# Position terms taken out of the compression's input and added to its product; the two widest HGRN2 spans subtracted by ScalarE's bias

## The chip, the cores and the metric

The kernel runs on one core of a Trainium2 chip. Five engines work side by side: TensorE (PE) multiplies, VectorE (DVE) and ScalarE (ACT) work element by element, GpSimd (POOL) issues the indirect gathers, and SyncE (SP) issues nearly all other transfers. The metric is the device time of one execution in microseconds (us).

## The reference, cut to what matters

One decoder layer over 1024 tokens of width 1024: RMSNorm, one wide input projection, three parallel mixers (stick-breaking attention, native sparse attention with a compressed, a selected and a sliding branch, HGRN2 recurrence), a gated merge, then a PEER expert layer with 16384 experts, and a last RMSNorm. Two places of it are touched:

```python
# native sparse attention: keys and values compressed over blocks of 32 tokens, stride 16
def compress(x, w):
    pieces = x.reshape(B, G, n_piece, CMP_STRIDE, dh)
    blocks = jnp.concatenate([pieces[:, :, j:j + n_cmp] for j in range(per)], axis=3) + cmp_pe
    return blocks.reshape(B, G, n_cmp, CMP_LEN * dh) @ w

# HGRN2, inside one chunk: the decay between two times
b = jnp.cumsum(gc, axis=2)
rel = b[:, :, :, None, :] - b[:, :, None, :, :]
decay = jnp.exp(jnp.where(causal[:, :, None], rel, -jnp.inf))
```

`cmp_pe` is one array of 32 x 64 position terms, the same for every block, so `(blocks + cmp_pe) @ w` is `blocks @ w` plus one vector of 64 numbers.

## The kernel before, in words

The tokens go through in four parts of 256. For each part the kernel writes out the normalisation, the projections (`proj`: 24 matmuls per block of 128 columns, each operand split into two fp16 halves), and the *items* of the mixers, which are stepped through a four-stage software pipeline: for each part and each of four rounds one HGRN2 head (`hg_items`), one tile of sparse attention (`nsa_items`) and one pair of stick-breaking heads (`sb_items`). The other work (projections, merges, output projection, PEER scores and routes) is cut into pieces, and a planner places them between the items: it adds up a modelled DVE and PE load of what has been written so far (`account`) and keeps each at so much per step (`RDVE`, `RPE`). The tile framework then schedules all of it by a timeline of its own, and that fixes the order of each engine's queue. So an edit of a few instructions moves many others.

PEER is done in two ways. Parts 1 and 2 (512 tokens) are computed densely, in 128 blocks of experts, after the mixers (`gemm1`, `gemm2`, here *the dense stage*). Each block takes 24 matmuls of 512 columns into `g`, 18 into the six `acc` banks, and every fourth block 24 more for the seventh and eighth bank, whose sum DVE adds at L1451. Parts 0 and 3 (512 tokens, four tiles of 128) go by gathers: POOL fetches for each of 128 ranks one row of 4 KB per token, 0.524 MB in all, first from the table `u` (L1149, multiplied by DVE at L1151), then from `v` (L1159, accumulated by DVE at L1161 into `gacc`). That makes 1024 gathers and 1024 DVE instructions. 420 of them are spread over the mixers' steps by `paced`, and the rest are left to the scheduler in the dense stage. A gather row needs a free buffer, so a gather is issued when DVE has finished with an earlier row.

The changed places:

- `pieces(which)`, for keys (0) and values (1) of each part. `plain` projects the block and ACT copies it out of PSUM into `xc` (L486). `add_pe` then lets DVE write `xp`, of 16 position pairs by group by compressed block, with the position term added, in four instructions (group by parity) for each half of the 32 positions (L510), and four small ones for the piece carried over from the part before (`xhist`, stored at L521). Every token is written twice, once in each half.
- `compress(which, dst)`: 16 fp32 matmuls over `xp` into `pk` (L526), copied by DVE into `kcT` or `vcT` (L527).
- `level(lv)` of `hg_items`, seven levels for each of 16 head-parts. For level `lv` the 256 columns are cut into spans of `2w`, `w = 2**lv`; `spans` subtracts from each span the value of `b` at its middle, by one DVE instruction of 128 x 256 (L806), and ACT takes the absolute value (L807) and the exponential (L808).

The order of queues that matters for what follows: each engine works through its own queue in order; DVE's queue in the mixers holds HGRN2, attention, route and gather instructions mixed, and in the dense stage the weight splits `us` and `vs` (L221), the gating `ge` (L1434), the split `ac`, the bank sums and the gathers' instructions.

## Time and profile before

| what | us |
|---|---|
| median of 3 runs | 3500.18 (3494.5 to 3507.36) |
| the profiled execution | 3511.97 |
| its span, first to last instruction | 3510.2 |
| PE busy | 3199.7 |
| DVE busy | 3000.6 |
| ACT busy | 1556.4 |
| POOL busy | 1361.7 |

The profiled execution took 1.8 us more than its span, and 11.8 us more than the median of the runs. Mean granted TensorE clock: 0.942. Times within the trace count from the span's start. In rows of windows, what stands behind each stretch is its length, then the busy time of each engine with the number of instructions, the granted clock, the mean busy share of the 16 DMA engines, and GB/s. In rows of groups, the count is followed by the busy time of all, the mean of one in ns, and the idle time of the engine just before them with what ended it.

### The profile page before, as it was taken

To read this page: it belongs to the slowest core of one execution; us is meant where nothing else is said; L and a number is where in the kernel's file an instruction comes from. 1 tells how busy PE (TensorE), PEld (TensorE's weight loads), DVE (VectorE), ACT (ScalarE), POOL (GpSimd) and SP (SyncE) were. 2 spreads that over 40 slices of the span, in tenths; PEclk is the share of its full clock that TensorE was granted. 3 is DMA by queue.
4 is the path that set the end of the run, shared out by engine and by line. 5 is a ranking of instruction groups with operands and counts; after the bars stand their busy time and mean duration, and the time that the engine had idled before them with its cause. 6 is when DMAs were issued, how large, how long until landed. Compare 5 with 4: busy or idle time off the path is not lost.

```text
span 3510.2 us, 56907 instructions
## 1 busy us (share of the span) xinstructions
PE 3199.7 (91%) x20564; PEld 2175.3 (62%) x20564; DVE 3000.6 (85%) x6666; ACT 1556.4 (44%) x3181; POOL 1361.7 (39%) x1170
## 2 busy tenths in 40 slices
PE   7999889999997799999887889889999999999998
PEld 6887777778886688888565745434444444444443
DVE  6665679888789879889997869999988998998998
ACT  5776455554543554554455233333333333333333
POOL 0000002443332322333231334357765565676672
PEclk9999999999997799999688999989999999999999
DMA  8964856889976588897574998789999999999995
GB/s 305 334 248 147 308 185 226 320 314 310 358 284 231 199 289 291 327 332 259 191 250 154 344 372 312 241 271 387 392 384 329 385 367 362 362 368 375 367 358 219
DMA packets 359283, 1058.00 MB, mean 301 GB/s; under 512 B 35236, under 2 KB 107573, under 8 KB 354391
## 3 DMA queue, kind: packets, MB, share of 16 engines
q0 software_dynamic: 147456, 536.94, 42.5%
q1 hardware_dynamic: 206934, 483.87, 38.7%
q10 hardware_dynamic: 4608, 33.56, 2.5%
q8 instruction: 161, 2.64, 0.3%
q14 instruction: 124, 1.01, 0.1%
HBM read 944.13 MB, written 110.10 MB: 300 GB/s over the span
## 4 chain that ended last, share of the span: by engine, by line
PE 49%; DVE 23%; DMA 11%; issue 8%; ACT 6%; POOL 2%; SPq 0%; DVEq 0%; POOLq 0%; ACTq 0%
PE g L265 13%; PE acc L1441 10%; PE pj_mg L265 4%; DVE u L1151 3%; DVE gacc L1161 3%; PE g L1441 3%; DMA u<-in_peer_u_dram,gidx 3%; PE pj_r_hg L265 2%; DMA v<-in_peer_v_dram,gidx 1%; PE pb L265 1%; DMA gt<-d_G 1%; PE pj_wo L265 1%; POOL v L1159 1%; PE z_sb L417 1%; DMA vraw<-in_peer_v_dram 1%
## 5 line engine op out<-in xcount | busy, mean ns | idle before, releaser
L1159 POOL DMA_INDIRECT v<-in_peer_v_dram,gidx x421 | 556.0, 1321 | 674.0 <-DVE gacc L1161 348.4
L1149 POOL DMA_INDIRECT u<-in_peer_u_dram,gidx x417 | 529.7, 1270 | 596.6 <-DVE u L1151 367.4
L265 PE MATMUL g<-h,us 128*128 128x512 f16 x3072 | 688.2, 381 | 14.8 <-ACT ge L1400 12.1
L1441 PE MATMUL acc<-vs,ac 128*128 128x512 f16 x2304 | 542.2, 383 | 39.9 <-ACT vs L220 23.5
L1441 PEld LDWEIGHTS <-ac 128*128 128x128 f16 x3072 | 303.1, 99 | 426.1 <-issue 66.8
L1161 DVE SCALAR_TENSOR_TENSOR gacc<-v,act,gacc 128x1024 f32<-128x1024 f32 x421 | 538.9, 1280 | 29.4 <-DMA v<-in_peer_v_dram,gidx 25.8
L265 PEld LDWEIGHTS <-us 128*128 128x128 f16 x3072 | 301.6, 98 | 383.0 <-issue 21.1
L1151 DVE SCALAR_TENSOR_TENSOR u<-u,gh 128x1024 f32<-128x1024 f32 x417 | 501.9, 1219 | 33.2 <-DMA u<-in_peer_u_dram,gidx 32.7
L1400 ACT ACTIVATE ge<-g 128x512 f32<-128x512 f32 x128 | 76.1, 596 | 520.7 <-PE g L265 500.1
L265 PE MATMUL pj_mg<-hT,w_mg 128*128 128x256 f16 x2304 | 273.8, 275 | 4.0 <-ACT mg L885 4.0
L265 PEld LDWEIGHTS <-w_mg 128*128 128x128 f16 x2304 | 228.2, 100 | 33.6 <-issue 6.6
L1441 PE MATMUL g<-vs,ac 128*128 128x512 f16 x768 | 190.5, 388 | 11.6 <-ACT ge L1400 11.6
L1149 POOL DMA_INDIRECT rr_u<-in_peer_u_dram,gidx x95 | 134.2, 1413 | 96.7 <-DVE rr_u L1151 49.8
L221 DVE SCALAR_TENSOR_TENSOR vs<-vraw,vs 128x1024 f16<-128x1024 f32 x128 | 154.1, 1219 | 18.6 <-ACT vs L220 18.5
L221 DVE SCALAR_TENSOR_TENSOR us<-uraw,us 128x1024 f16<-128x1024 f32 x128 | 156.1, 1219 | 10.4 <-ACT us L220 10.3
L265 PE MATMUL pb<-o,w_b 128*128 128x256 f16 x1152 | 144.7, 281 | 21.1 <-DVE sg L923 15.1
L1159 POOL DMA_INDIRECT rr_v<-in_peer_v_dram,gidx x90 | 123.0, 1367 | 102.2 <-DVE gacc L1161 81.4
L220 ACT ACTIVATE vs<-vraw 128x1024 f16<-128x1024 f32 x128 | 131.0, 1046 | 55.0 <-DMA vraw<-in_peer_v_dram 55.0
L220 ACT ACTIVATE ac<-ge 128x512 f16<-128x512 f32 x128 | 79.9, 628 | 168.3 <-DVE ge L1434 139.0
L1434 DVE TENSOR_TENSOR ge<-ge,gt 128x256 f32<-128x256 f32 x256 | 98.4, 422 | 58.7 <-ACT ge L1400 44.9
L1223 PE MATMUL gb<-hot 128*128 128x128 f16 x512 | 125.7, 294 | 24.3 <-ACT stage L1226 13.1
L220 ACT ACTIVATE us<-uraw 128x1024 f16<-128x1024 f32 x128 | 134.2, 1048 | 21.4 <-PE g L265 12.8
(1146 smaller groups left out, 6353.8 us busy)
## 6 DMA issues: line engine op xcount, KB each, us to landing
uraw<-in_peer_uT_dram SPq DMA_DIRECT2D x128, 512.0 KB, 7.7
vraw<-in_peer_v_dram SPq DMA_DIRECT2D x128, 512.0 KB, 7.2
w_mg<-dw SPq DMA_DIRECT2D x72, 512.0 KB, 5.8
gt<-d_G SPq DMA_DIRECT2D x32, 1024.0 KB, 17.5
d_G<-stages ACTq DMA_DIRECT2D x20, 1024.0 KB, 5.9
w_r_hg<-dw SPq DMA_DIRECT2D x36, 512.0 KB, 5.4
w_b<-dw SPq DMA_DIRECT2D x72, 256.0 KB, 5.5
wr_mg<-in_wblk_dram SPq DMA_DIRECT2D x24, 512.0 KB, 5.3
```

Source lines behind the costliest of these rows:

```text
L220: S.activation(hi, src, AF.Copy, scale=scale)
L221: V.scalar_tensor_tensor(lo, in0=src, scalar=scale, in1=hi, op0=ALU.mult, op1=ALU.subtract)
L265: P.matmul(ps, l[:, k, :], r[:, k, :], start=(i == 0), stop=(i == n - 1))
L417: P.matmul(x["z"], qz[:, hh, tl * 128:(tl + 1) * 128], st["k"][:, r0 + c0:r0 + c1], start=True, stop=(c0 > 0))
L1149: G.indirect_dma_start(out=ur, out_offset=None, in_=a["peer_u"], in_offset=bass.IndirectOffsetOnAxis(ap=idx[:, c:c + 1], axis=0))
L1151: V.scalar_tensor_tensor(ur, in0=ur, scalar=1.0, in1=h2, op0=ALU.mult, op1=ALU.mult, accum_out=hpre[:, c:c + 1])
L1159: G.indirect_dma_start(out=vr, out_offset=None, in_=a["peer_v"], in_offset=bass.IndirectOffsetOnAxis(ap=idx[:, c:c + 1], axis=0))
L1161: V.scalar_tensor_tensor(acc, in0=vr, scalar=act[:, c:c + 1], in1=acc, op0=ALU.mult, op1=ALU.add)
L1223: P.matmul(ps[:, n, :], hs[:, 0, :, n], hs[:, 2, :, n], start=True, stop=False)
L1400: S.activation(ge, ps, AF.Gelu, scale=1.0 / (SW * SH2))
L1434: V.tensor_tensor(gv, gv, gt[:, :, i % 8, :], op=ALU.mult)
L1441: P.matmul(ps, ac[:, x, t * 128:(t + 1) * 128], v[:, y, dh * 512:(dh + 1) * 512], start=start and n == 0, stop=stop and n == 2)
```

## The change

The position terms are laid out on the host as 16 columns of 128 (`pos`) in place of 32 columns of 64 written twice. `pieces` keeps its projection in PSUM, and ACT writes it straight into `xp` with four instructions of 64 x 8 x 16; `xp` now holds each token once (8 position pairs, one column more), and the matmuls of the second half read it one column further on. The carried piece is copied by ACT, in and out of `xhist`. On the first part the 16 weight blocks are also multiplied with `pos` (16 more matmuls of one column for keys, 16 for values), DVE copies the result to `cpos`, and the copy of `pk` becomes an addition of `cpos`. In `level`, where there are four spans or fewer (levels 5 and 6), ACT computes the absolute difference itself, one instruction for each span with the middle value as its bias.

The words given for the change name a third part, ranks decoded by eleven VectorE operations. The diff holds no edit of the decoding: in both kernels `route` decodes with the same 26 instructions per tile (L1038 to L1052 before).

```diff
-    small = load(cst.tile([128, 40], F32, name="small"), a["small"])
-    peT, hnorm, hlb = small[:, 0:32], small[:, 32:36], small[:, 36:40]
+    small = load(cst.tile([128, 24], F32, name="small"), a["small"])
+    pos, hnorm, hlb = small[:, 0:16], small[:, 16:20], small[:, 20:24]
...
-    xhist = per.tile([128, 2, 16], F32, name="xhist")
+    xhist = per.tile([128, 2, 8, 2], F32, name="xhist")
+    cpos = per.tile([64, 2], F32, name="cpos")
...
         def pieces(which):
-            plain(B_NKV + which, f"xc{which}")
-            xc = st[f"xc{which}"]
-            xp = st["xp", which] = W2(f"xp{which}_{nm}", (128, 16, 2, np_), tag="xp", bufs=1)
-
-            def add_pe(half, d0, nb, src):
-                for g in range(2):
-                    gs = slice(g * 64, g * 64 + 64)
-                    for par in range(2):
-                        o = xp[par * 64:par * 64 + 64, half * 8:half * 8 + 8, g, d0:d0 + nb]
-                        i = src[gs].rearrange("p (c j u) -> p u j c", j=8, u=2)[:, par]
-                        e = peT[gs, half * 16:half * 16 + 16].rearrange("p (j u) -> p u j", u=2)[:, par]
-                        V.tensor_tensor(o, i, e.unsqueeze(2).to_broadcast([64, 8, nb]), op=ALU.add)
-            if pt.first:
-                add_pe(0, 0, np_ - 1, xc[:, 0:n - 16])
-                add_pe(1, 0, np_ - 1, xc[:, 16:n])
-            else:
-                add_pe(0, 0, 1, xhist[:, which, :])
-                add_pe(0, 1, np_ - 1, xc[:, 0:n - 16])
-                add_pe(1, 0, np_, xc)
+            ps = proj(B_NKV + which, hTs[pt.i], f"xc{which}_{nm}", pt)
+            d0 = 0 if pt.first else 1
+            xp = st["xp", which] = W2(f"xp{which}_{nm}", (128, 8, 2, np_ + 1), tag="xp", bufs=1)
+            if not pt.first:
+                S.activation(xp[:, :, :, 0], xhist[:, which], AF.Copy)
+            for g in range(2):
+                for par in range(2):
+                    o = xp[par * 64:par * 64 + 64, :, g, d0:d0 + np_]
+                    S.activation(o, ps[g * 64:g * 64 + 64].rearrange("p (c j u) -> p u j c", j=8, u=2)[:, par], AF.Copy, scale=PS)
             if not pt.last:
-                V.tensor_copy(xhist[:, which, :], xc[:, n - 16:n])
+                S.activation(xhist[:, which], xp[:, :, :, d0 + np_ - 1], AF.Copy)
 
         def compress(which, dst):
             pk = ps_mm.tile([64, 2, np_], F32, tag="mm", name=f"pk{which}_{nm}")
             for j in range(16):
-                P.matmul(pk[:, :, 0:ncb], st["cw", which][:, j, :], st["xp", which][:, j, :, 0:ncb], start=(j == 0), stop=(j == 15))
-            V.tensor_copy(dst[0:64, :, c0:c1], pk[:, :, 0:ncb])
+                P.matmul(pk[:, :, 0:ncb], st["cw", which][:, j, :], st["xp", which][:, j % 8, :, j // 8:j // 8 + ncb], start=(j == 0), stop=(j == 15))
+            if pt.first:
+                pc = ps_mm.tile([64, 1], F32, tag="mm", name=f"pc{which}")
+                for j in range(16):
+                    P.matmul(pc, st["cw", which][:, j, :], pos[:, j:j + 1], start=(j == 0), stop=(j == 15))
+                V.tensor_copy(cpos[:, which:which + 1], pc)
+            V.tensor_scalar(dst[0:64, :, c0:c1], pk[:, :, 0:ncb], cpos[:, which:which + 1], None, op0=ALU.add)
...
             def spans():
                 y["X"] = X = W2(f"X{lv}_{nm}", (128, n))
-                b4 = halves(x["b"])
-                V.tensor_tensor(halves(X), b4, b4[:, :, 0:1, w - 1:w].to_broadcast([128, ns, 2, w]), op=ALU.subtract)
-                S.activation(X, X, AF.Abs)
+                if ns <= 4:
+                    for i in range(0, n, 2 * w):
+                        S.activation(X[:, i:i + 2 * w], x["b"][:, i:i + 2 * w], AF.Abs, scale=-1.0, bias=x["b"][:, i + w - 1:i + w])
+                else:
+                    b4 = halves(x["b"])
+                    V.tensor_tensor(halves(X), b4, b4[:, :, 0:1, w - 1:w].to_broadcast([128, ns, 2, w]), op=ALU.subtract)
+                    S.activation(X, X, AF.Abs)
                 S.activation(X, X, AF.Exp, scale=-1.0)
```

The queues are scheduled anew, and three places of them are shown. In the rows a tile's name ends in the number of its buffer, and the lines of the changed kernel are up to six lower for the same statement (one higher near L221).

First, DVE in part 2, at the compression of the keys. `xc` and `xp` are the projection and its rearranged copy, `u` a gathered row, `o` and `e_sb` belong to the attention of part 1. Before:

```order
L1151 SCALAR_TENSOR_TENSOR u_70_32828,hpre_32615<-u_70_32828,gh_0_32609 128x1024
L510 TENSOR_TENSOR xp_ns_9666<-xc_ns_9664,small 64x8x15 x4
L510 TENSOR_TENSOR xp_ns_9666<-xc_ns_9664,small 64x8x16 x4
L521 COPY xhist<-xc_ns_9664 128x16
L1151 SCALAR_TENSOR_TENSOR u_71_32831,hpre_32615<-u_71_32831,gh_0_32609 128x1024
L429 SCALAR_TENSOR_TENSOR e_sb_1_1_0_0_9531<-r_sb_1_1_0_0_9534,e_sb_1_1_0_0_9531 128x512
L221 SCALAR_TENSOR_TENSOR o_1_7834<-tro_ns1g_0_9542,o_1_7834 128x256
L1151 SCALAR_TENSOR_TENSOR u_72_32834,hpre_32615<-u_72_32834,gh_0_32609 128x1024
L221 SCALAR_TENSOR_TENSOR o_1_7834<-tro_ns1g_1_9547,o_1_7834 128x256
L527 COPY kcT<-pk_ns_9744 64x2x16
L510 TENSOR_TENSOR xp_ns_9820<-xhist,small 64x8 x4
```

And in the change:

```order
L1149 SCALAR_TENSOR_TENSOR u_75_32846,hpre_32618<-u_75_32846,gh_0_32612 128x1024
L1149 SCALAR_TENSOR_TENSOR u_76_32849,hpre_32618<-u_76_32849,gh_0_32612 128x1024
L222 SCALAR_TENSOR_TENSOR o_1_7853<-tro_ns1g_0_9565,o_1_7853 128x256
L222 SCALAR_TENSOR_TENSOR o_1_7853<-tro_ns1g_1_9570,o_1_7853 128x256
L430 SCALAR_TENSOR_TENSOR e_sb_1_1_0_0_9554<-r_sb_1_1_0_0_9557,e_sb_1_1_0_0_9554 128x512
L433 TENSOR_TENSOR r_sb_1_1_0_0_9557<-z_sb_1_1_0_0_9553,e_sb_1_1_0_0_9554 128x512
L521 TENSOR_SCALAR kcT<-pk_ns_9783,cpos 64x2x16
L430 SCALAR_TENSOR_TENSOR e_sb_1_1_1_0_9695<-r_sb_1_1_1_0_9698,e_sb_1_1_1_0_9695 128x512
```

All of `xp` and `xhist` is gone from DVE, and the gathers' instructions stand four further on at the same point (`u_76` where `u_72` stood).

Second, ACT in part 2, at the spans of head 2 (`X_hg_2`, one buffer for each level; `b_hg_2` is the running sum). Before, all seven levels read as the last two do here:

```order
L807 ACTIVATE X_hg_2_9935<-X_hg_2_9935 128x256
L837 ACTIVATE kd_hg_2_10216<-b_hg_2_9777 128x128
L807 ACTIVATE X_hg_2_9977<-X_hg_2_9977 128x256
L807 ACTIVATE X_hg_2_10044<-X_hg_2_10044 128x256
L807 ACTIVATE X_hg_2_10082<-X_hg_2_10082 128x256
L807 ACTIVATE X_hg_2_10153<-X_hg_2_10153 128x256
L808 ACTIVATE X_hg_2_9935<-X_hg_2_9935 128x256
```

And in the change:

```order
L805 ACTIVATE X_hg_2_9839<-X_hg_2_9839 128x256
L806 ACTIVATE X_hg_2_9839<-X_hg_2_9839 128x256
L460 ACTIVATE o_sb_1_9852<-ov_sb_1_9706 128x256
L801 ACTIVATE X_hg_2_10058<-b_hg_2_9769 128x64 x4
L801 ACTIVATE X_hg_2_10160<-b_hg_2_9769 128x128 x2
L805 ACTIVATE X_hg_2_9883<-X_hg_2_9883 128x256
L504 ACTIVATE xp_ns_15504<-xhist 128x16
L806 ACTIVATE X_hg_2_10058<-X_hg_2_10058 128x256
```

The two widest levels (buffers 10058 and 10160) have come forward, ahead of four narrower ones, since they no longer wait for DVE.

Third, the end of DVE's queue, from the last splits of expert weights (`vs`) to the first output row (`yd`). `gacc` is the accumulator of the last gathered tile, `v_n` or `rr_v_n` the gathered row of rank n. Before:

```order
L1161 SCALAR_TENSOR_TENSOR gacc_35338<-v_125_35693,act_34974,gacc_35338 128x1024
L1451 TENSOR_TENSOR acc_23020<-acc_23020,p_123_4_32341 128x512
L1161 SCALAR_TENSOR_TENSOR gacc_35338<-rr_v_126_35696,act_34974,gacc_35338 128x1024 x2
L221 SCALAR_TENSOR_TENSOR vs_32384<-vraw_32382,vs_32384 128x1024
L221 SCALAR_TENSOR_TENSOR vs_32412<-vraw_32410,vs_32412 128x1024
L232 TENSOR_SCALAR gms_fin_35706<-gss_fin_35703 128x1
L1434 TENSOR_TENSOR ge_32350<-ge_32350,gt_0_32111 128x256
```

And in the change:

```order
L1159 SCALAR_TENSOR_TENSOR gacc_35341<-v_122_35687,act_34977,gacc_35341 128x1024
L1159 SCALAR_TENSOR_TENSOR gacc_35341<-v_123_35690,act_34977,gacc_35341 128x1024
L222 SCALAR_TENSOR_TENSOR vs_32475<-vraw_32473,vs_32475 128x1024
L1159 SCALAR_TENSOR_TENSOR gacc_35341<-v_124_35693,act_34977,gacc_35341 128x1024
L1159 SCALAR_TENSOR_TENSOR gacc_35341<-v_125_35696,act_34977,gacc_35341 128x1024
L1159 SCALAR_TENSOR_TENSOR gacc_35341<-rr_v_126_35699,act_34977,gacc_35341 128x1024
L1468 SCALAR_TENSOR_TENSOR yd_32441<-acc_22988,yd_32441 128x512
L1468 SCALAR_TENSOR_TENSOR yd_32441<-acc_22989,yd_32441 128x512
L1159 SCALAR_TENSOR_TENSOR gacc_35341<-rr_v_126_35699,act_34977,gacc_35341 128x1024
L1468 SCALAR_TENSOR_TENSOR yd_32471<-acc_22990,yd_32471 128x512
```

Before, the last gather stood ahead of the last four splits; now gathers stand up to the first output row, and one stands behind it. Counted over the whole queue, the gathers' instructions ahead of the eighth bank's sum (the second of a pair of L1451, named by its block) are:

| ahead of the sum of block | 3 | 19 | 55 | 119 | 123 | end |
|---|---|---|---|---|---|---|
| before | 434 | 506 | 671 | 1000 | 1022 | 1024 |
| change | 440 | 518 | 679 | 984 | 1005 | 1024 |

ACT's queue holds 91 table loads before and 84 in the change; DVE's holds 124 instructions fewer.

More of the change, by code (lines that the diff above doesn't have):

```diff
@@ L1538, in _layout @@
     pe = np.asarray(inp["nsa_cmp_pe"])[0].T
-    small = [np.concatenate([pe, pe], axis=0), np.asarray(inp["hgrn_norm"])[0].reshape(4, 128).T, np.asarray(inp["hgrn_lower_bounds"])[0].reshape(4, 128).T]
+    small = [pe.reshape(64, 16, 2).transpose(2, 0, 1).reshape(128, 16), np.asarray(inp["hgrn_norm"])[0].reshape(4, 128).T, np.asarray(inp["hgrn_lower_bounds"])[0].reshape(4, 128).T]
     d["small"] = np.ascontiguousarray(np.concatenate(small, axis=1))
```

## The prediction

> **What bounds the kernel now.** I read the busy shares first, then the chain that ended last, then the engines by stretch. PE is busiest, yet only half of the chain is PE; DVE has a quarter of it, ACT little.
>
> ```profile
> PE 3199.7 (91%) x20564; PEld 2175.3 (62%) x20564; DVE 3000.6 (85%) x6666; ACT 1556.4 (44%) x3181; POOL 1361.7 (39%) x1170
> PE 49%; DVE 23%; DMA 11%; issue 8%; ACT 6%; POOL 2%; SPq 0%; DVEq 0%; POOLq 0%; ACTq 0%
> ```
>
> The windows show that the bound changes with the stage. The columns after the length are PE, PEld, DVE, ACT and POOL.
>
> ```profile
> 0.00:90.00 90.00, 64.10 (x535) 55.54 (x535) 55.55 (x130) 50.55 (x103) 5.39 (x43) 0.92 0.83 301
> 90.00:440.00 350.00, 325.94 (x2832) 287.13 (x2831) 214.18 (x526) 226.23 (x562) 2.76 (x26) 0.97 0.73 259
> 440.00:610.00 170.00, 154.73 (x1247) 130.25 (x1247) 144.84 (x651) 94.19 (x202) 15.63 (x22) 0.98 0.60 207
> 610.00:1050.00 440.00, 409.46 (x3286) 349.81 (x3285) 371.90 (x945) 228.23 (x570) 169.90 (x179) 0.95 0.89 317
> 1050.00:1235.00 185.00, 146.91 (x924) 119.86 (x922) 174.34 (x546) 77.25 (x204) 60.93 (x58) 0.74 0.64 217
> 1235.00:1590.00 355.00, 343.13 (x2812) 298.24 (x2811) 303.30 (x632) 196.23 (x463) 105.82 (x114) 0.98 0.87 308
> 1590.00:2040.00 450.00, 366.38 (x2479) 295.30 (x2478) 399.52 (x1100) 193.13 (x423) 136.43 (x119) 0.83 0.71 246
> 2110.00:2349.00 239.00, 208.12 (x1012) 103.48 (x1010) 227.62 (x640) 73.99 (x102) 104.44 (x73) 0.94 0.81 271
> 2349.00:2722.00 373.00, 373.00 (x1730) 169.12 (x1729) 343.44 (x526) 128.26 (x171) 252.81 (x174) 1.00 1.00 370
> 2722.00:3063.00 341.00, 330.92 (x1524) 149.23 (x1523) 313.77 (x393) 112.67 (x149) 207.37 (x154) 0.99 0.99 368
> 3063.00:3428.00 365.00, 342.96 (x1553) 153.20 (x1551) 338.81 (x429) 112.91 (x149) 258.34 (x176) 0.98 0.99 368
> 3428.00:3490.00 62.00, 62.00 (x289) 28.14 (x288) 53.36 (x61) 20.51 (x28) 20.19 (x16) 1.00 0.66 242
> ```
>
> From 90 to 440 and 1235 to 1590 PE is busy 93% and 97%; there a DVE instruction less buys little. From 1050 to 1235 and 1590 to 2040 DVE is the fuller engine (94%, 89%), PE is at 79% and 81%, and the granted clock falls to 0.74 and 0.83. In the dense stage PE fills 2349 to 2722; from 2722 to 3428 it loses 32 us while the DMA engines move 368 GB/s, hardly less than their 370 with PE full: transfers are at their limit there.
>
> **DVE's part.** What goes:
>
> ```profile
> L806 DVE TENSOR_TENSOR X_hg<-b_hg 128x256 f32<-128x256 f32 x112 | 40.1, 419 | 0.5
> L510 DVE TENSOR_TENSOR xp_ns<-xc_ns,small 64x120 f32<-64x120 f32 x40 | 14.1, 352 | 2.5 <-ACT xc_ns L486 2.0
> L510 DVE TENSOR_TENSOR xp_ns<-xc_ns,small 64x128 f32<-64x128 f32 x24 | 8.7, 364 | 0.4
> L510 DVE TENSOR_TENSOR xp_ns<-xhist,small 64x8 f32<-64x8 f32 x24 | 4.0, 165 | 0.2
> L521 DVE COPY xhist<-xc_ns 128x16 f32<-128x16 f32 x6 | 1.1, 176 | 0.2
> ```
>
> Two of seven levels, 32 of 112 subtractions: 32 x 0.419 = 13.4. The position terms: 14.1 + 8.7 + 4.0 + 1.1 = 27.9. Together 41.3 us of DVE, all of it in the mixers. The two copies to `cpos` add under 0.4, and the addition in place of the copy of `pk` nothing to speak of. Not all of it counts. In the four stretches with DVE at 84% or more lie
>
> ```profile
> 440.00:610.00 170.00, 2.61 (x7) 0.98 0.60 207
> 610.00:1050.00 440.00, 9.95 (x28) 0.95 0.89 317
> 1050.00:1235.00 185.00, 5.13 (x14) 0.74 0.64 217
> 1590.00:2040.00 450.00, 5.03 (x14) 0.83 0.71 246
> ...
> 610.00:1050.00 440.00, 7.04 (x24) 0.95 0.89 317
> ```
>
> 22.7 us of L806 (the first four rows, DVE's time on that line), of which two sevenths are 6.5, and 7.0 us of L510 (the last row, from the same view of that line): 13.5 us. I take 9, two thirds of it, also about DVE's 23% of the chain times 41.3 us. The bounds are 0 (PE hides all) and 41.
>
> **ACT's part.** A 128 x 128 instruction with a bias column and one of 128 x 64 stand in the trace, and so do copies from PSUM on both sides of the new 64 x 8 x 16 ones:
>
> ```profile
> L807 ACT ACTIVATE X_hg<-X_hg 128x256 f32<-128x256 f32 x112 | 43.1, 410 | 29.9 <-DVE X_hg L806 29.9
> L837 ACT ACTIVATE kd_hg<-b_hg 128x128 f32<-128x128 f32 x32 | 11.2, 393 | 4.8 <-DVE ua_rt L1027 3.4 <-PE pa_hg L822 1.4
> L587 ACT ACTIVATE s_ns1g0t<-s_ns1g0t,mx_ns1g0t 128x64 f32<-128x64 f32 x8 | 2.7, 336 | 2.5 <-DVE mx_ns1g0t L583 2.5
> L486 ACT ACTIVATE xc_ns<-pj_xc_ns 128x256 f32<-128x256 f32 x8 | 3.1, 385 | 8.8 <-PE pj_xc_ns L265 8.8
> L421 ACT ACTIVATE e_sb<-z_sb 128x128 f32<-128x128 f32 x16 | 4.3, 271 | 2.5 <-PE ov_sb L447 1.2 <-PE z_sb L417 0.8 <-PE z_sb L419 0.3
> L539 ACT ACTIVATE gts_ns<-tr_ng_ns 128x48 f32<-128x48 f32 x2 | 0.4, 212 | 0.0
> L902 ACT ACT_TABLE_LOAD x26 | 33.4, 1283 | 0.8 <-ACT stages L1226 0.4
> 59.33 4.38 PE L265 MATMUL pj_xc_ns<-hT,w_xc_ns 128*128 128x256 f16 x24
> 55.19 1.47 PE L526 MATMUL pk_ns<-xp_ns,cw_ns 128*64 128x30 f32 x16 [0.35 <-DVE xp_ns L510]
> ```
>
> Level 6: 32 x 0.393 = 12.6. Level 5: 64 x 0.336 = 21.5. The new copies: 32 at 0.271 (128 elements from PSUM) to 0.385 (256); with the strided order unseen I take 0.28, nearest to the row of equal count: 9.0, at most 12.3. Twelve small ones at 0.212: 2.5. Gone: 32 x 0.410 = 13.1 and 3.1. Net +29.4. Seven table loads fewer at 1.283 take off 9.0: +20.4 us on an engine that has 6% of the chain: 1 us, bounds 0 and 20. What hides it is PE or DVE at 84% and more from 90 on; uncovered it costs its 20. A head's levels 5 and 6 wait for ACT alone: 4 x 0.336 against 0.419 + 0.410 before is half a us later for level 5, but the products are a later step. ACT's 29.9 us of waiting for L806 shrink by up to two sevenths, 8.5.
>
> The Trainium skill (ScalarE: Activation LUTs, section Rules for kernel authors) speaks against this move: it gives additions to VectorE, not ScalarE. The rows agree on the price, 34.1 us of ACT for levels 5 and 6 in place of 13.4 on DVE and 13.1 on ACT; read so, the sum would lose its gain in the mixers. The same page (section What ACT_TABLE_LOAD costs) puts a switch of tables at about 2.66 us with its drain, where the row shows 1.283; by the page the seven loads would be worth 18.6, an estimate, and ACT would carry nearly 11 us.
>
> **PE's part.** The position product is 2 x 16 matmuls of one column. The last row above has sixteen of the same weights and 30 columns at 1.47: at most 2.9 us, once, before 90, where PE is idle 26 of 90. I take 0. The projection's PSUM bank is held by four ACT instructions, 4 x 0.28, in place of one of 0.385; the next projection has the other bank for its 4.38 us, which hides the 0.7.
>
> The mixers: -9 + 1 = **-8 us**, between -41 and +23 (ACT and PE uncovered, nothing gained).
>
> **The dense stage moves too.** No instruction of it is edited, but its gathers stand elsewhere. By the count of the queue, at the sum of block 19 the change has done 12 more (518 for 506), between blocks 19 and 55 four fewer (161 for 165), between 55 and 119 24 fewer (305 for 329), after 119 16 more (40 for 24).
>
> ```profile
> L1161 DVE SCALAR_TENSOR_TENSOR gacc<-v,act,gacc 128x1024 f32<-128x1024 f32 x421 | 538.9, 1280 | 29.4 <-DMA v<-in_peer_v_dram,gidx 25.8
> 2349.32 0.68 DVE L1451 TENSOR_TENSOR acc<-acc,p 128x512 f32<-128x512 f32 x1
> 2722.01 0.68 DVE L1451 TENSOR_TENSOR acc<-acc,p 128x512 f32<-128x512 f32 x1
> 3427.67 0.68 DVE L1451 TENSOR_TENSOR acc<-acc,p 128x512 f32<-128x512 f32 x1
> L1441 PE MATMUL acc<-vs,ac 128*128 128x512 f16 x2304 | 542.2, 383 | 39.9 <-ACT vs L220 23.5 <-DVE vs L221 8.7 <-ACT ac L220 4.1
> ```
>
> The three times are the seventh bank's sums of blocks 19, 55 and 119.
> - Early: 12 x 1.28 = 15.4 us of DVE into 239 us where DVE idles 11.4: between 4.0 and 15.4 later; I take +10.
> - 19 to 55: PE is full, 372.7 us for nine groups of four blocks, 41.4 each. Nothing.
> - 55 to 119: 16 such groups would take 662 and took 705.7, 43 us more. 24 gathers of 0.524 MB are 12.6 MB, 34 us at 368 GB/s. Of `acc`'s 39.9 us of waits 23.5 come through ACT's split from late transfers. I take -22, bounds 0 and -34.
> - After 119: 16 x 1.28 = 20.5 us of DVE into 62 us where it idles 8.6, less the split and the gather that now stand elsewhere (2.5): up to +9; I take +7, from 0 to 12.
>
> Together **-5**, between -30 and +27. The sum is -13 on 3511.97, so 3499; that execution lay 11.8 above the median, and the same -13 on 3500.2 gives **3487**.
>
> **The rivals.**
> *DVE and transfers count in full.* For it: DVE at 84 to 94% in four stretches, DMA at 0.99. The 13.5 us, all 34 in the middle, the ends at their least (+4, 0): -43.5, 3457. Against: PE at 93% to 97% in two stretches.
> *Hidden.* PE sets the pace and the ends cancel the middle: 3500.
> *Slower by where the gathers went.* If the middle's loss is PE's and DVE's own and not the transfers', the fewer gathers there buy nothing, while the early stage (DVE 95% busy) and the tail pay: 15.4 + 12 = +27, 3527. It decides once the middle gives back less than about 19 us. Against it: 368 GB/s on both sides of 3063.
> *ScalarE late.* Its +20.4 uncovered with DVE's share hidden: 3520. For it: ACT is at 65% from 90 to 440. Against: 6% of the chain. The Trainium skill's rule on additions, named above, would have it so.
> *Not what it says.* The third part in the words isn't in the diff. Were eleven decoding instructions left of 26, 15 x 8 tiles at 0.22 to 0.30
>
> ```profile
> L1046 DVE TENSOR_SCALAR ua_rt<-fa_rt 128x128 uint32<-128x128 f32 x24 | 5.3, 220 | 0.0
> L1049 DVE COPY_PREDICATED fb_rt<-ua_rt,fa_rt 128x128 f32<-128x128 uint32 x24 | 7.2, 299 | 0.3
> ```
>
> would take some 29 us more off DVE, two thirds of it on the path: 3468.
>
> **How the numbers follow.** Within 0.5% (17.5 us; about what can be told from no change) means 3482.7 to 3517.7. The forecast has 0.43, itself 3472 to 3502: 0.16 faster, 0.26 same, 0.01 slower. In full: 0.21, faster. Hidden: 0.15 (0.14 same, 0.01 slower). Gathers: 0.14 (0.13 slower, 0.01 same). ScalarE: 0.05 (0.04 slower, 0.01 same). Eleven: 0.02, faster. That makes faster 0.39, same 0.42, slower 0.19. The range 3452 to 3526 leaves out the better half of *in full* and the worse half of *gathers*, some 0.17.
>
> **What would show it.** DVE's busy sum 41 lower, ACT's 20 higher, 32 `xp` instructions on ACT near 0.28 and level 5's four near 0.336. The start of the dense stage about 8 us earlier; block 19's sum no earlier than before; the time from 55 to 119 near 684 for 706, PE busier there; PE's last `acc` some 7 us further behind block 119's sum. If the dense stage starts over 20 us earlier, DVE counted in full; if 55 to 119 stays at 706, the transfers weren't the limit; if ACT waits less and PE waits more for `pk`, ScalarE was late. A median over 3526 or under 3452 makes the forecast wrong.

## The result, and the profile after

The changed kernel takes 3546.8 us (median; 3545.1 to 3550.7), the kernel before beside it 3501.9: a ratio of 1.0131, 95% interval 1.0110 to 1.0152. It is slower, and outside the forecast's range (3452 to 3526). In the table of runs further down, one of e6's four executions, 5502.3 us at a granted clock of 0.613 (0.935 to 0.940 in the other three), is left out. The profiled execution has a span of 3544.9 us for 3510.2. Busy sums and the engines of the chain that ended last, after:

```profile
PE 3206.5 (90%) x20628; PEld 2187.7 (62%) x20628; DVE 2973.2 (84%) x6542; ACT 1567.9 (44%) x3274; POOL 1367.6 (39%) x1170
PE 52%; DVE 23%; DMA 9%; issue 8%; ACT 6%; POOL 2%; SPq 0%; POOLq 0%; DVEq 0%; ACTq 0%
```

DVE is 27.4 us less busy, ACT only 11.5 more, and the span is 35 longer: no engine has more work that would account for it. PE's share of the chain rose from 49% to 52%, DMA's fell from 11% to 9%. The edited instructions cost what the nearest rows had promised. Groups by shape, after:

```profile
L804 DVE TENSOR_TENSOR X_hg<-b_hg 128x256 f32<-128x256 f32 x80 | 29.2, 422 | 0.5
L805 ACT ACTIVATE X_hg<-X_hg 128x256 f32<-128x256 f32 x80 | 30.2, 408 | 14.5 <-DVE X_hg L804 14.4
L801 ACT ACTIVATE X_hg<-b_hg 128x64 f32<-128x64 f32 x64 | 17.0, 340 | 6.0 <-DVE X_hg L813 3.6 <-DVE b_hg L776 1.7 <-PE pa_hg L820 0.7
L801 ACT ACTIVATE X_hg<-b_hg 128x128 f32<-128x128 f32 x32 | 11.1, 391 | 3.3 <-PE pa_hg L820 3.2
L508 ACT ACTIVATE xp_ns<-pj_xc_ns 64x128 f32<-64x128 f32 x32 | 8.8, 276 | 10.4 <-PE pj_xc_ns L266 10.1
L813 DVE TENSOR_TENSOR X_hg<-X_hg,raw_hg 128x256 f32<-128x256 f32 x112 | 44.8, 431 | 9.4 <-ACT X_hg L806 9.0
```

The last one's counterpart before:

```profile
L815 DVE TENSOR_TENSOR X_hg<-X_hg,raw_hg 128x256 f32<-128x256 f32 x112 | 44.6, 431 | 0.6 <-ACT X_hg L808 0.5
```

0.340, 0.391 and 0.276 us stand where 0.336, 0.393 and 0.28 were forecast. ACT's waiting for DVE's subtractions fell from 29.9 to 14.4, and some of it came back as a new wait: DVE, at the next step, waits 9.0 us for the exponentials in place of 0.5.

Where the time went is read from instructions that both kernels have. From the timelines: ACT's square of an HGRN2 head's output (`sq_hg`, the 11th and the 16th of 16), and DVE's sum of the seventh bank for block 3. Before:

```profile
1103.31 0.38 ACT L862 ACTIVATE sq_hg<-ov_hg 128x256 f32<-128x256 f32 x1 [1.81 <-PE ov_hg L854]
...
1838.62 0.38 ACT L862 ACTIVATE sq_hg<-ov_hg 128x256 f32<-128x256 f32 x1
...
2114.71 0.68 DVE L1451 TENSOR_TENSOR acc<-acc,p 128x512 f32<-128x512 f32 x1
```

After, with the sums of blocks 19, 55 and 119 as well:

```profile
1106.39 0.39 ACT L860 ACTIVATE sq_hg<-ov_hg 128x256 f32<-128x256 f32 x1 [2.65 <-PE ov_hg L852]
...
1861.32 0.38 ACT L860 ACTIVATE sq_hg<-ov_hg 128x256 f32<-128x256 f32 x1
...
2158.31 0.69 DVE L1449 TENSOR_TENSOR acc<-acc,p 128x512 f32<-128x512 f32 x1
...
2405.02 0.68 DVE L1449 TENSOR_TENSOR acc<-acc,p 128x512 f32<-128x512 f32 x1
...
2773.46 0.68 DVE L1449 TENSOR_TENSOR acc<-acc,p 128x512 f32<-128x512 f32 x1
...
3452.12 0.68 DVE L1449 TENSOR_TENSOR acc<-acc,p 128x512 f32<-128x512 f32 x1
```

| at | later than before, us |
|---|---|
| 11th head, part 2 | 3.1 |
| 16th head, part 3 | 22.7 |
| block 3 | 43.6 |
| block 19 | 55.7 |
| block 55 | 51.4 |
| block 119 | 24.5 |
| end of the span | 34.7 |

Nearly all of the loss is made in the mixers and at their end, between 1103 and 2115 of before: 40 us there. The dense stage gave back 9, for a forecast of 5.

### The profile page after: what moved, and what is told of

The parts are those of the page before. It is cut to its first block, busy times and chain, and to the rows that moved or that the text cites. A ratio compares the mean times of both kernels' runs of the same rounds, so it can differ in the third digit from the quotient of the medians.

```text
span 3544.9 us, 57024 instructions
## 1 busy us (share of the span) xinstructions
PE 3206.5 (90%) x20628; PEld 2187.7 (62%) x20628; DVE 2973.2 (84%) x6542; ACT 1567.9 (44%) x3274; POOL 1367.6 (39%) x1170
## 4 chain that ended last, share of the span: by engine, by line
PE 52%; DVE 23%; DMA 9%; issue 8%; ACT 6%; POOL 2%; SPq 0%; POOLq 0%; DVEq 0%; ACTq 0%
PE g L266 14%; PE acc L1439 11%; PE pj_mg L266 4%; DVE u L1149 4%; DVE gacc L1159 3%; PE g L1439 3%; DMA v<-in_peer_v_dram,gidx 3%; DMA u<-in_peer_u_dram,gidx 2%; PE pb L266 2%; PE pj_r_hg L266 2%; PE pj_wo L266 2%; DMA gt<-d_G 1%; POOL u L1147 1%; DMA vraw<-in_peer_v_dram 1%; DVE e_sb L430 1%
## 5 line engine op out<-in xcount | busy, mean ns | idle before, releaser
L1157 POOL DMA_INDIRECT v<-in_peer_v_dram,gidx x421 | 541.1, 1285 | 737.0 <-DVE gacc L1159 401.9
L1147 POOL DMA_INDIRECT rr_u<-in_peer_u_dram,gidx x95 | 141.6, 1491 | 86.1 <-DVE rr_u L1149 54.9
L221 ACT ACTIVATE ac<-ge 128x512 f16<-128x512 f32 x128 | 79.7, 627 | 194.1 <-DVE ge L1432 155.4
L222 DVE SCALAR_TENSOR_TENSOR us<-uraw,us 128x1024 f16<-128x1024 f32 x128 | 155.9, 1219 | 11.5 <-ACT us L221 10.0
L221 ACT ACTIVATE vs<-vraw 128x1024 f16<-128x1024 f32 x128 | 132.5, 1047 | 73.7 <-DMA vraw<-in_peer_v_dram 73.6
L1157 POOL DMA_INDIRECT rr_v<-in_peer_v_dram,gidx x90 | 130.8, 1454 | 80.4 <-DVE gacc L1159 53.8
L221 ACT ACTIVATE us<-uraw 128x1024 f16<-128x1024 f32 x128 | 134.2, 1048 | 22.9 <-PE g L266 18.8
```

What stands on the lines that cost most here:

```text
L221: S.activation(hi, src, AF.Copy, scale=scale)
L222: V.scalar_tensor_tensor(lo, in0=src, scalar=scale, in1=hi, op0=ALU.mult, op1=ALU.subtract)
L1147: G.indirect_dma_start(out=ur, out_offset=None, in_=a["peer_u"], in_offset=bass.IndirectOffsetOnAxis(ap=idx[:, c:c + 1], axis=0))
L1157: G.indirect_dma_start(out=vr, out_offset=None, in_=a["peer_v"], in_offset=bass.IndirectOffsetOnAxis(ap=idx[:, c:c + 1], axis=0))
```

## The experiments

One thing of the program matters for all of them. Pieces (projections, gates, merges, routes, and the 128 `spread` pieces that write the gates of the dense stage to DRAM) are placed by the planner: after every step it emits more of them until the load it has added up in `load_` has reached what the step allows. The change takes DVE work out of what is added up, so the planner places pieces elsewhere: 285 of 748 move, 147 to earlier steps and 138 to later ones, 174 of them by a single step, and 122 of the 128 spread pieces are among them. Gathers move along: the program shares the 420 paced ones among the steps by PE's modelled load in each, and 195 of them fall to another step, by one or two. The theory that came from this: **the moved pieces carry the loss, not the edited instructions**. The rivals: ScalarE's longer work is late; the compressed product is; any new order made by the scheduler costs some tens of microseconds.

Adding to `load_` by hand moves pieces without touching an instruction, or keeps them in place although instructions go. All runs (the ratio is to the kernel before, run beside them on the same chip):

| run | edits | pieces as in | us | ratio, 95% interval |
|---|---|---|---|---|
| e1 | spans | its own plan | 3580.1 | 1.0209 (1.0175 to 1.0243) |
| e2 | compression | its own plan | 3539.2 | 1.0094 (1.0063 to 1.0125) |
| e3 | both | before | 3521.1 | 1.0046 (1.0028 to 1.0064) |
| e4 | none | the change | 3542.4 | 1.0106 (1.0080 to 1.0132) |
| e5 | none | 24 us more charged | 3532.3 | 1.0081 (1.0059 to 1.0104) |
| e6 | none | half the change's charge | 3545.9 | 1.0104 (1.0073 to 1.0135) |
| e7 | both | rate 2.94 | 3558.6 | 1.0139 (1.0111 to 1.0167) |
| e8 | both, ScalarE lighter | before | 3526.8 | 1.0060 (1.0034 to 1.0085) |
| e9 | none | the change, to step 290 | 3529.1 | 1.0082 (1.0056 to 1.0108) |
| e10 | none | the change, from step 290 | 3537.4 | 1.0093 (1.0067 to 1.0119) |
| e11 | both, 440 gathers | before | 3520.3 | 1.0040 (1.0024 to 1.0056) |
| e12 | both | as e5 | 3546.1 | 1.0122 (1.0102 to 1.0143) |
| f1 | spans | before | 3510.2 | 0.9992 (0.9974 to 1.0009) |
| f2 | compression | before | 3518.1 | 1.0016 (0.9997 to 1.0035) |
| f3 | eight memsets | before | 3508.7 | 0.9997 (0.9979 to 1.0015) |
| f4 | none | as e5, to step 290 | 3533.6 | 1.0071 (1.0043 to 1.0099) |

The kernel before had medians of 3505.2 (e1 to e4), 3504.8 (e5 to e8), 3504.4 (e9 to e12) and 3511.9 (f1 to f4).

### Each half with its own plan: e1, e2

e1 is the kernel before with the edit of `spans` alone; e2 is the changed kernel with `spans` as before.

> The kernel before with the two widest spans alone on ScalarE; the position terms stay on VectorE. If ScalarE's longer work is what the mixers pay (levels 5 and 6 take 34.1 us of it for 13.1 before), most of the 45 us is here: 3530 or more. If the loss comes with the compressed product, about 3500. If it comes from the planner, which charges VectorE 10 us less here and moves pieces for it, some of it, 3510 to 3530.

> The changed kernel with all seven spans back on VectorE; the position terms in the product stay. If ScalarE's spans carry the loss: about 3495 (VectorE has 28 us less). If the compressed product carries it (its PSUM bank held by four instructions, the product later): 3530 or more. If the planner does: between the two, and 3510 to 3530 if the loss grows with what is moved.

3580 and 3539. Both lie above the 3510 to 3530 that the theory of the pieces had, and taken alone each fits the rival for its own half. But both halves lose, and e1, a part of the edits, loses more than the whole change, by some 27 us if the ratios are compared. A cost that sits in instructions doesn't fall when more of them are added, so ScalarE's spans aren't refuted by this, but they can't be all of it.

### The plan and the edits apart: e3, e4

e3, the change, with the planner charged for what was removed:

```diff
+            load_["DVE"] += 8 * 0.06 + 8 * 8 * (np_ - 1) / 960.0 if pt.first else 12 * 0.06 + 4 * 8 * 2 * np_ / 960.0
+            if not pt.last:
+                load_["DVE"] += 0.06 + 16 / 960.0
...
+                load_["DVE"] -= 0.06 + 1 / 960.0
+                load_["PE"] -= 16 * 4 / 2400.0
...
                 if ns <= 4:
+                    load_["DVE"] += 0.06 + n / 960.0
```

With it all 748 pieces stand in before's steps. e4 is the kernel before with the same terms and opposite signs: all 748 stand in the change's.

> The changed kernel with every edited instruction, but the planner charged as if VectorE still had the removed ones, so that all 748 pieces stand in the steps in which they stood before. If the moved pieces carry the loss: 3490, from 3480 to 3502, what the prediction would have had for the mixers. If ScalarE's instructions themselves do, the new steps don't matter: 3540 to 3550. If any change of order at all costs some tens of us: anywhere between.

> The kernel before, no instruction edited, but the planner charged as in the change, so that the pieces stand in the change's steps. If the moved pieces carry the loss: 3540 to 3565 (the loss without VectorE's relief). If the edited instructions carry it: 3495 to 3505.

e4, in which no instruction is edited, loses 37 us; e3, in which all are, 16. So the pieces carry most of the loss, and e3's 16, between the outcomes expected of it, are left to the edits and their own order of the queues. In e4 the loss even stands where the change has it (11th head, 16th head, blocks 3 and 119; timelines of e4):

```profile
1100.05 0.38 ACT L870 ACTIVATE sq_hg<-ov_hg 128x256 f32<-128x256 f32 x1 [2.97 <-PE ov_hg L862]
...
1861.11 0.38 ACT L870 ACTIVATE sq_hg<-ov_hg 128x256 f32<-128x256 f32 x1
...
2159.47 0.69 DVE L1459 TENSOR_TENSOR acc<-acc,p 128x512 f32<-128x512 f32 x1
...
3447.84 0.68 DVE L1459 TENSOR_TENSOR acc<-acc,p 128x512 f32<-128x512 f32 x1
```

-3, +22, +45, +20, beside the change's +3, +23, +44, +24. In e3's trace the heads and block 3 stand at -7, +0.5 and +8:

```profile
1096.28 0.39 ACT L866 ACTIVATE sq_hg<-ov_hg 128x256 f32<-128x256 f32 x1 [1.81 <-PE ov_hg L858]
...
1839.13 0.38 ACT L866 ACTIVATE sq_hg<-ov_hg 128x256 f32<-128x256 f32 x1
...
2122.62 0.69 DVE L1455 TENSOR_TENSOR acc<-acc,p 128x512 f32<-128x512 f32 x1
```

So the mixers' 44 us come with the moved pieces and the gathers that move along. No run moves the pieces and holds the gathers. e11 below moves 407 of the paced gathers, most of them by over two steps, without a piece, and isn't slower than e3, so the gathers alone are the less likely carrier; that the pieces are it without them isn't shown. The granted clock isn't it: over the whole execution PE is busy 3190.4 us in e4, 3199.7 before. What the loss looks like on the engines is seen in e4, whose instructions are those of before. Windows from the 12th head of HGRN2 to the last pair of stick-breaking heads, and from the output projection of part 3 (its third block) to block 3's sum (columns as before); before:

```profile
1243.00:1936.00 693.00, 622.26 (x4593) 518.16 (x4590) 609.96 (x1582) 361.37 (x825) 204.34 (x201) 0.90 0.75 260
2008.00:2115.00 107.00, 90.57 (x513) 52.51 (x511) 77.43 (x106) 43.85 (x64) 40.17 (x29) 0.92 0.99 356
```

e4:

```profile
1244.00:1967.00 723.00, 632.50 (x4662) 528.91 (x4659) 622.13 (x1591) 360.26 (x828) 218.52 (x204) 0.89 0.73 255
2038.00:2159.00 121.00, 93.13 (x508) 52.83 (x507) 79.73 (x104) 42.82 (x61) 41.50 (x33) 0.86 0.91 329
```

The first stretch is 30 us longer. PE idles 90.5 us of it for 70.7 before, and DVE 100.9 for 83.0, 18 to 20 more each; the other 10 to 12 are more work that falls into it (69 matmuls more on PE). No single wait carries it. Waits of DVE in the mixers, before (to 2099) and e4 (to 2144):

```profile
DVE e_sb L429 <- ACT e_sb L424: 30.9, 20, 4.0
DVE hot L1219 <- PE gb L1224: 25.9, 27, 4.5
DVE gacc L1161 <- DMA v<-in_peer_v_dram,gidx: 19.7, 17, 2.6
```

```profile
DVE e_sb L429 <- ACT e_sb L424: 46.2, 26, 5.4
...
DVE hot L1227 <- PE gb L1232: 30.0, 27, 4.5
DVE gacc L1169 <- DMA v<-in_peer_v_dram,gidx: 27.9, 23, 3.2
```

and PE's in e4, none of which is in PE's list of before at 4 us or more:

```profile
PE pa_hg L830 <- DVE att_hg L835: 12.8, 8, 5.2
...
PE acc L1449 <- ACT ac L220: 10.7, 1, 10.7
PE pj_wo L265 <- ACT stage L1234: 10.6, 1, 10.6
...
PE tr_n L282 <- DVE ht_n L291: 8.8, 2, 4.6
```

Stick-breaking attention waits longer for ACT (+15 us), gathers for transfers (+8), the spread pieces for PE (+4), HGRN2's matmuls for DVE, and at the end of the mixers the last gates (`stage`) and the first `ac` come late, 10.6 and 10.7 in one piece each. Other waits shrank (PE's `gb` for the gates from 13.1 to 5.1), so part of this is waiting that has only moved.

### Is it a rule, or the plan's luck: e5, e6, e7

e5 and e6 are e4 with its terms multiplied by -1 and by 0.5. e7 is the change with one number edited:

```diff
-RPE, RDVE, REND, PD = 3.5, 3.0, 5.0, 1.2
+RPE, RDVE, REND, PD = 3.5, 2.94, 5.0, 1.2
```

> The kernel before, no instruction edited, but the planner charged with 24 us more of VectorE work in place of 24 less, so that pieces move the other way (spread pieces of the second spread 2 steps later, gates of part 1 up to 5 earlier). If pulling pieces forward is what costs: 3490 to 3510, no loss. If before's plan is simply a good one among many and any other is worse: 3520 to 3550, as with 24 less.

> The kernel before with the planner charged 12 us less, half of what the change takes off. If the loss goes with the amount taken off: 3520 to 3527, half of the 37 us. If it is luck of the plan: anywhere from 3495 to 3550, with no relation to the half.

> The change with every edit, and the planner's allowance for VectorE lowered with its work, from 3.00 to 2.94 a step. The plan is the change's up to step 300 (parts 0 and 1), while the spread of part 1 then stands where it did before, and that of part 2 two or three steps later. If the spread pieces' earlier places carry the loss: 3505 to 3525, near the change with before's plan (3521). If the part before step 300 does: 3540 to 3550.

More charged loses 28 us, and half of the change's charge as much as the whole (1.0104 beside 1.0106). The lower rate, meant to bring the spread pieces back, is the worst of the three: 3558.6, where 3505 to 3525 was expected if they were the cause. So neither the direction nor the amount sets the loss. The plans don't lose at the same place either. In e5 the mixers are even faster; 16th head and block 3 of its timeline stand 10 us earlier and 8 later than before,

```profile
1828.63 0.38 ACT L870 ACTIVATE sq_hg<-ov_hg 128x256 f32<-128x256 f32 x1
...
2122.40 0.69 DVE L1459 TENSOR_TENSOR acc<-acc,p 128x512 f32<-128x512 f32 x1 [0.42 <-ACT p L1458]
```

and its profiled span is 17 us longer: here most is lost from the end of the mixers on. In the other plans of the unedited kernel block 3 is late already, by 45 us in e4, 35 in e6, 14 and 30 in e9 and e10, and 19 in f4.

### Early or late pieces: e9, e10, f4

e9 and e10 are e4 with its DVE terms counted only up to step 290 (`* (stepped[0] < 290)`) or only from there; f4 is e5 up to step 290.

> The kernel before, no instruction edited, with the change's places only for the pieces up to step 290 (parts 0 and 1 and the routes of part 1; 151 of 748 pieces move, 19 of them spread pieces). By the anchors of the full shift (3542, 11 us late by the middle of part 2, 31 at its end) it should lose 5 to 12 us: 3510 to 3517. If every other plan is worse by the same 30 us: 3530 to 3550.

> The counterpart: before's places up to step 290, then the change's (143 pieces move, 109 of them spread pieces, nearly all one to ten steps earlier). If the spread pieces' earlier places carry the loss: 3528 to 3540. If every other plan is worse by the same 30 us, that is also what this shows, and then the early one must show it too. If the loss is made early: 3500 to 3512.

> The kernel before with the planner charged 24 us a kernel more, but only up to step 290: in the fully charged run part 2 began 22 us sooner, and the 25 us were lost in the dense stage. If that gain can be had alone: 3480 to 3500, better than before. If any departure from before's plan costs, as the six plans so far: 3520 to 3550.

25, 33 and 22 us slower. The two halves of one plan, 151 and 143 pieces, lose more together (58) than the whole (37), so the time can't be assigned to pieces and summed. At block 3 it nearly could be: the profiled executions of e9 and e10 are 13.5 and 30.0 late there, together 43.5, and e4's is 44.8. What doesn't add up is the dense stage, in which e4 gets 15 us back, e10 6 and e9 nothing. These are single executions, and the runs of one kernel spread by 5 to 25 us. The early gain of e5 wasn't had alone: f4's 16th head is 12 us late, where e5's is 10 early.

### ScalarE's part, and VectorE's relief: e8, e11, e12

e8 is e3 with one instruction for all spans of a level, so that the differences of all but the first span are left out:

```diff
-                    for i in range(0, n, 2 * w):
-                        S.activation(X[:, i:i + 2 * w], x["b"][:, i:i + 2 * w], AF.Abs, scale=-1.0, bias=x["b"][:, i + w - 1:i + w])
+                    S.activation(X, x["b"], AF.Abs, scale=-1.0, bias=x["b"][:, w - 1:w])
```

e11 is e3 with `PACE` at 440 for 420. e12 is the change with e3's terms doubled, which puts all pieces into e5's steps.

> The change in before's plan (3521), but each of levels 5 and 6 written by one ScalarE instruction of 128 x 256 with one bias, in place of four and two; the differences of all spans but the first are left out of the computation that way, and ScalarE has about 21 us less. If ScalarE's longer work is what takes back VectorE's relief: 3495 to 3505. If ScalarE is covered, as the prediction counted it: 3516 to 3524.

> The change in before's plan (3521), with 440 gathers paced over the mixers' steps in place of 420: 20 x 1.28 is 25.6 us, the VectorE time that the change freed. If that time is really free in the mixers: the dense stage has 20 x 0.524 MB less to bring in, 28 us at 368 GB/s, and the time falls to 3493 to 3508. If it isn't: the mixers lose what the dense stage gains, 3515 to 3525, or more.

> The change in the plan that the kernel before had with 24 us more charged (3532 there, but its mixers ended 7 us earlier than before's and the dense stage lost 25). If VectorE's relief counts nothing, as with before's plan: 3530 to 3545. If each pair of plan and instructions has its own luck: anywhere from 3495 to 3560.

e8 isn't faster than e3 (1.0060 and 1.0046), but it tests less than it was meant to. Its row, and the two rows of e3 in whose place it stands:

```profile
L806 ACT ACTIVATE X_hg<-b_hg 128x256 f32<-128x256 f32 x32 | 15.1, 505 | 11.0 <-PE pa_hg L825 7.3 <-DVE b_hg L781 3.7
```

```profile
L807 ACT ACTIVATE X_hg<-b_hg 128x64 f32<-128x64 f32 x64 | 17.4, 341 | 4.3 <-DVE b_hg L781 3.0 <-PE pa_hg L826 1.1
L807 ACT ACTIVATE X_hg<-b_hg 128x128 f32<-128x128 f32 x32 | 11.2, 393 | 3.0 <-PE pa_hg L826 3.0
```

That is 13.5 us less, where 21 was expected, and with 101 table loads for e3's 93 ScalarE's whole sum is only 1.2 us lower (1581.0 for 1582.2). So e8 doesn't settle whether ScalarE is late in e3. f1, below, answers it for the spans alone. e12 is 14 us slower than the unedited kernel in the same plan, as e3 is 16: the two parts of the loss add up roughly, and the edits, VectorE's relief among them, gain nothing in either plan. e11 gains nothing, but not for the reason expected. Its dense stage starts as late as e3's (both 8 us after before), with some 453 gathers done for 434 by the count of the trace, so DVE's freed time in the mixers was indeed free. The dense stage made nothing of it. Windows from block 19 to 55, 55 to 119, and to the end; e3:

```profile
2358.00:2735.00 377.00, 374.47 (x1728) 169.27 (x1727) 343.97 (x527) 128.03 (x170) 255.24 (x175) 1.00 0.99 367
2735.00:3425.00 690.00, 670.98 (x3072) 301.87 (x3071) 633.59 (x804) 225.41 (x298) 429.31 (x316) 0.99 0.98 366
3425.00:3519.00 94.00, 73.08 (x331) 32.55 (x329) 82.92 (x108) 30.15 (x49) 34.89 (x30) 0.90 0.69 255
```

e11:

```profile
2356.00:2741.00 385.00, 379.87 (x1747) 171.45 (x1746) 338.52 (x500) 126.72 (x168) 239.61 (x168) 0.99 0.96 355
2741.00:3431.00 690.00, 667.01 (x3061) 300.35 (x3060) 619.72 (x795) 221.36 (x295) 437.73 (x307) 0.99 0.96 356
3431.00:3523.00 92.00, 69.69 (x313) 30.84 (x311) 82.65 (x107) 27.04 (x46) 40.01 (x31) 0.90 0.71 264
```

From block 55 to 119 both take 690 us, although by the count of the trace e11 has 306 gathers there and e3 317. From 19 to 55 e11 takes 8 us more, 5 of them PE's own busy time. The transfers run at 355 GB/s for 367. With PE busy in 97 to 99% of both stretches and fewer gathers left to bring in, it isn't shown whether less was asked for or less was delivered.

### Each edit in before's plan, and a control: f1, f2, f3

f1 and f2 are e1 and e2 with e3's terms for what each removes; in f3 the kernel before gets, ahead of each copy of `pk`, an instruction that nothing needs, with its charge taken off again:

```diff
+            V.memset(cpos, 0.0)
+            load_["DVE"] -= 0.06 + 2 / 960.0
             V.tensor_copy(dst[0:64, :, c0:c1], pk[:, :, 0:ncb])
```

> Levels 5 and 6 on ScalarE alone, all 748 pieces in before's steps. The same edit with its own plan took 3580. If the plan carries that: 3495 to 3520. If ScalarE's instructions do: 3560 or more. If the 16 us of the whole change in before's plan (3521) are the spans': 3515 to 3525; if they are the compression's: 3498 to 3508.

> The compressed product alone, in before's steps. With its own plan it took 3539. If the plan carries that: 3490 to 3520. If the 16 us of the whole change in before's plan are the compression's: 3515 to 3525; if they are the spans': 3490 to 3505.

> A control: the kernel before in its own plan, with eight instructions of VectorE added that nothing needs (a memset of 64 x 2 ahead of each copy of the compressed product, some 0.1 us each). If an edit costs what its instructions take: within 5 us of before, 3499 to 3509. If the scheduler's order alone, made anew for any added instruction, is worth 10 us or more: outside of that, up or down.

The spans that took 3580 with their own plan take 0.9992 of before in before's, with ScalarE busy 1567.7 us for 1556.4: the 2% come with the plan, and the move from DVE to ScalarE costs nothing net in before's. Whether the unedited kernel would lose as much in that plan wasn't run. The compression costs 0.16%, with an interval that reaches to nothing. The control turned out to tell less than was expected of it: the scheduler put all eight instructions at the head of DVE's queue, and left the order of every other row on DVE, PE and ACT as it was. What it shows is how closely two equal kernels compare (0.9997). It is f1 and f2 that answer the question of the order: of the some 4800 rows of DVE's queue, about 1300 stand elsewhere or are changed in f1, 1000 in f2 and 1450 in e3, beside 2050 in e4 and 2400 in the change. A new order of over a thousand rows, with the pieces in place, cost nothing in f1.

f1's profiled execution even looks like the gain that the forecast had for the mixers (16th head, blocks 3, 19 and 119 of f1):

```profile
1826.66 0.38 ACT L867 ACTIVATE sq_hg<-ov_hg 128x256 f32<-128x256 f32 x1
...
2107.97 0.69 DVE L1456 TENSOR_TENSOR acc<-acc,p 128x512 f32<-128x512 f32 x1
...
2348.95 0.69 DVE L1456 TENSOR_TENSOR acc<-acc,p 128x512 f32<-128x512 f32 x1
...
3419.12 0.68 DVE L1456 TENSOR_TENSOR acc<-acc,p 128x512 f32<-128x512 f32 x1
```

It is 12 us earlier at the 16th head and 6.7 at block 3, 0.4 at block 19, 8.6 at block 119 and 3.2 at the end of the span. That is one execution, of a kernel whose ten runs spread by 16 us; over the runs nothing is left of it that can be measured.

Taken together: the six runs without a piece moved (e3, e8, e11, f1, f2, f3) stand at 0.9992 to 1.0060. The six of the unedited kernel in other plans stand at 1.0071 to 1.0106, and those of the change, whole or half, in other plans (the change, e1, e2, e7, e12) at 1.0094 to 1.0209. No version was faster than the kernel before.

## Why the prediction was wrong, point by point

**The step that failed is the mixers' term, -8 us with bounds of -41 and +23.** It summed the edited instructions, ACT's and DVE's, stretch by stretch, as if everything between them stayed where it was. Measured: +44 at block 3. The upper bound failed for the same reason, since it let every edited instruction be uncovered and no other one move. What was missing is a term for the pieces that the planner moves, and e4, with those pieces moved and no instruction edited, puts it at 45 us at that place. The working had the queues in hand and priced what moved in the dense stage by counting it there; in the mixers it looked at the edited places alone.

**What the edits cost by themselves** was closer to right. In before's plan the spans are worth 0.9992 and the compression 1.0016; both together 1.0046, some 16 us, which neither half shows alone. Where that comes from is open: e8 took too little off ScalarE to tell, and e3's own order of the queues is as good a candidate. Of DVE's 9 us that the forecast counted, f1's runs show nothing.

**DVE's busy sum** was to fall by 41.3 and fell by 27.4. The rows of the position terms that went add up to 27.9, as forecast, and those of the spans to 40.1 - 29.2 = 10.9, not 13.4: the 13.4 multiplied a count by the mean duration, and neighbours on DVE overlap. The timeline of before shows it on three comparisons in a row, 0.68 us each and 0.60 apart:

```profile
2006.34 0.68 DVE L1219 TENSOR_TENSOR hot<-iorep,spread 128x1024 f16<-128x1024 f16 x1
2006.95 0.68 DVE L1220 TENSOR_TENSOR hot<-hot,spread 128x1024 f16<-128x1024 f16 x1
2007.55 0.68 DVE L1219 TENSOR_TENSOR hot<-iorep,spread 128x1024 f16<-128x1024 f16 x1
```

Of the 11 us that are still missing, some 7 may be what DVE's other work took in this plan: e4, with before's instructions, is 6.6 busier than before. The rest isn't accounted for. **ACT's sum** was to rise by 20.4 and rose by 11.5. The durations held, and two thirds of the difference is the same overlap: 64 x 0.340 is 21.8 where the row has 17.0, and 32 x 0.391 is 12.5 where it has 11.1. The seven table loads fewer, 9.0 us of the forecast, did come, but with the plan and not with the edits: there are 91 before, 84 in the change and 82 in e4, but 93 in e3. The Trainium skill's rule on additions (ScalarE: Activation LUTs, section Rules for kernel authors) gives them to VectorE. For the spans the time doesn't show a loss by the move: in before's plan it costs nothing (f1). That it gains nothing either agrees with the forecast's reading of the rule, by which the sum would lose its gain in the mixers.

**The dense stage**, forecast -5, came to -9, and by its own terms:

| stretch | forecast | measured |
|---|---|---|
| block 3 to 19 | +10 | +12.1 |
| 19 to 55 | 0 | -4.3 |
| 55 to 119 | -22 | -27.0 |
| after 119 | +7 | +10.3 |

The windows of the change for the two middle stretches:

```profile
2405.00:2773.00 368.00, 368.00 (x1706) 166.82 (x1705) 336.70 (x503) 121.69 (x161) 238.71 (x165) 1.00 0.99 365
2773.00:3452.00 679.00, 667.85 (x3082) 301.94 (x3081) 618.83 (x793) 225.44 (x299) 442.05 (x307) 0.99 0.98 363
```

PE is busy in 98% of the second, 95% before: with fewer gathers in it the stretch is shorter, as argued, at nearly the same 363 GB/s. The other traces bear this out: by their count the stretch takes 703 to 712 us with 328 to 330 gathers in it (724 in e1), 688 to 703 with 317 to 323, and 668 to 679 with 306. e11's 690 with 306 is the exception.

**The rivals.** *DVE and transfers in full* (3457) fell with the sign: the mixers gained nothing, and its -34 for the dense stage's middle was -27. *Hidden* (3500) is what f1 shows for the spans, not what the change does. *Slower by where the gathers went* (3527) had the sign right and the place wrong: the middle gave back 27, more than the 19 from which it would have been nothing. *ScalarE late* (3520) fell for the spans by f1. For both edits together it is open: e3 took 3521, ScalarE is 25.8 us busier in it than before, and e8 was too weak a test. *Not what it says*: the third part isn't in the code, as the diff had it. None of the rivals was the planner, though the section on the kernel before names its loads and says that an edit of a few instructions moves many others.

**What stays open** is why before's plan is better than the others. Six other plans, with 143 to 409 pieces moved, are all 0.7 to 1.1% slower on the same instructions. That its rates were set for just these loads would explain it; it is only argued. Nor do the traces give one wait whose removal would bring the 40 us back.

## What to carry to other kernels

Where a planner decides by the modelled load of what it has written, an instruction less is also an input to the planner: compare the two plans before any instruction is priced, and give the moved work a term of its own, here 22 to 41 us for plans in which most of the moved pieces moved by one to three steps, where the edits themselves cost some 16. To measure an edit apart from it, keep the plan by charging the planner for what was removed, and to measure the plan, charge it without the edit; the two together tell what the edits' own rows can't. A term worked out from mean durations is an upper bound where neighbours overlap: the row's busy time, not count times mean, is what goes.

## What the runs showed of the hardware that was not expected

Consecutive instructions overlap in the records, on DVE by 0.06 to 0.08 us (0.68 long and 0.60 apart; 112 x 0.419 = 46.9 in a row whose busy time is 40.1) and on ACT by some 0.1 (64 x 0.340 = 21.8 in a row of 17.0, mostly four in succession), so that many short instructions in a row cost less than their durations say. The number of ScalarE's table loads, 1.283 us each, follows from the order of its queue: 91 before and 82 in e4, with the same instructions, and 108 in e2.
